# A streaming encoder step on one core: where the sample's projection stands in TensorE's order within an ada block

## The chip, the cores and the metric

One Trainium2 chip, one core of it. The metric is device time in microseconds (us), lower is better; every time below is of that core. TensorE is PE in the profile, its weight loads PEld, VectorE DVE, ScalarE ACT, GpSimd POOL, SyncE SP (which issues the DMAs).

## What is computed

One layer of a hybrid encoder, for a prompt of 512 tokens and a sample of 64 tokens, width 2048, all in float32:

```python
shift, scale, gate = split(silu(c) @ W_ada + b_ada)          # one row for the prompt, one for the sample
h = rmsnorm(x) * (1 + scale) + shift
q, k, v, z_att, u_ssm, z_ssm, u_pool, z_pool = split(h @ W_in)
y = concat(rmsnorm(attention(q, k, v)) * silu(z_att),
           rmsnorm(s5(u_ssm)) * silu(z_ssm),
           rmsnorm(pool_mix(u_pool)) * silu(z_pool))
x = x + gate * (y @ W_out);  out = rmsnorm(x)
```

The change lies in the first stage, where shift, scale, h and the first six 128-wide tiles of `h @ W_in` are made.

## The kernel before, in words

Tokens lie along the free dimension, features on partitions: x is 16 blocks of 128 features by 576 tokens (512 prompt, 64 sample). A product with a large weight is made of three passes with the short float type: weight high times h high, weight low times h high, weight high times h low.

The first stage runs over the 16 feature blocks b (the loop at L447). Block b of h needs shift and scale of its own 128 features, and those need a product over all 2048 inputs: the **ada products** of block b, `ada_mm` (L324). They are 16 float32 matmuls, each with 32 columns of weights (silu(c), two columns of it in use) and 256 moving columns of W_ada; the sixteen are put on four column groups of the array (`pa[32 * g:...]`, L330), and each stands as two instructions in the trace, 32 in all. `ada_sel` (L333) copies the result out of PSUM (ScalarE, L336), transposes it in two matmuls (L338), adds the four groups with a VectorE reduce (L340) and makes scale and shift (L342, L343 through the helper at L73). `modulate` (L409) then makes block b of h: VectorE scales x (L419, helper L76) and makes `hs`, the sample's 64 columns (L421); ScalarE rounds to `hh` (L423); VectorE makes the rest `hl` (L425, helper L76).

`first_tiles(b, fs)` (L429) adds block b to the seven running sums. For f from 0 to 5 that is three matmuls with 128 weight columns and 512 moving columns (L436 to L438; tiles `fA`, `fB`, each of two halves, then `fC`, `fD`). For f = 6 it is the **sample's projection**: `hs` are the weights, in four groups of 32 columns, and 384 columns of W_in move (L442; four float32 matmuls, eight instructions, tile `fS`).

The order within a block is written out by hand: the loop stands under a manual schedule (L320) that keeps PE, SP, DVE and ACT in program order. `F1CUT` (L34) says which tiles stand in which of three places:

```python
        first_tiles(b, F1CUT[0])
        if b + 1 < KT:
            ada_mm(b + 1, 0)
            ada_mm(b + 1, 1)
        first_tiles(b, F1CUT[1])
        if b + 1 < KT:
            ada_sel(b + 1)
            modulate(b + 1)
        ...
        first_tiles(b, F1CUT[2])
```

So in block b stand, one after the other on PE, the tiles of `F1CUT[0]`, the ada products of block b + 1, the tiles of `F1CUT[1]`, the two transposes, the tiles of `F1CUT[2]`. Blocks 0 to 14 have ada products in them; block 15 has none.

Data: SP issues the ada tiles two blocks ahead (`load_ada`, L181, issued at L189: two of 1 MB for each block) and the block's 384 KB of W_in (`load_w1`, L174, issued at L178). An ada buffer is free again when the ada products that read it are done. ScalarE and VectorE split W_in into high and low ahead of the block (`split_w`, L379: `w1h` at L382, `w1l` through L70), and VectorE works off some of the scalar preparations of the S5 branch (`disc`, L247) at the end of each block. After the stage come attention, the S5 and pooling branches and the output projection, each with its own loops of three-pass matmuls (L500, L1118 to L1120).

Of the kernel before, what the change touches and what calls it, by code (L numbers as in the profile page):

```python
# [14 lines left out]
PSUM = bass.MemoryType.PSUM  # L15
# [17 lines left out]
PRE = 2  # L33
F1CUT = ((6, 0), (1,), (2, 3, 4, 5))  # L34
MANUAL = 0
# [13 lines left out]
def kernel(ctx, tc, xp, xs, xT, cT, wada_ss, wada_g, bsh, bsc, bgate, ng, wf1, wrest,  # L49
# [27 lines left out]

    # ---------------------------------------------------------------- constants
    ident = const.tile([128, 128], F32, name="ident")
# [20 lines left out]
    def rms_inv(pool, ssq, n, bias, hbias, shape, tag):  # L100
        """1/sqrt(ssq/n + bias), with a Newton step; hbias is -bias/2, bias may be None"""
        v = pool.tile(shape, F32, tag=tag + "v", name="v")
        s = pool.tile(shape, F32, tag=tag + "s", name="s")
        ts(v, ssq, -0.5 / n, hbias, ALU.mult, ALU.add)
        if bias is None:
            A.activation(s, v, AF.Sqrt, scale=-2.0)
        else:
            A.activation(s, ssq, AF.Sqrt, scale=1.0 / n, bias=bias)
        r = pool.tile(shape, F32, tag=tag + "r", name="r")
        V.reciprocal(r, s)  # L110
        mul(s, r, r)
        mul(s, s, v)
        stt(r, s, 1.5, r, ALU.add, ALU.mult)
        return r

    # ---------------------------------------------------------------- PSUM
    psctx = ExitStack()
# [5 lines left out]

    # ---------------------------------------------------------------- weights: loaded ahead, split into high and low
    wsrc = [wrest[r, :, 8 * h:8 * h + 8] for r in range(38) for h in range(2)]
# [34 lines left out]

    # ---------------------------------------------------------------- startup: x, modulation, first tiles
    hh, hl = [], []
# [183 lines left out]
    for b in range(PRE):  # L346
        load_ada(b)
    # 1/rms of each token, on every partition
    acc = [wp.tile([128, NT], F32, tag="wh", name="acc") for _ in range(2)]
# [14 lines left out]
    V.tensor_scalar(prm[:, 1], prm[:, 1], 1.0, None, op0=ALU.add)  # L364
    # keeps the array's clock up until the sums below
    warm = pp.tile([128, 2, 512], F32, tag="pj", name="warm")
# [62 lines left out]
    def first_tiles(b, fs):  # L429
        w, wh, wl, hs = blk[b]  # L430
        c, i = divmod(b, 4)
        f0, l0 = b == 0, b == KT - 1
        for f in fs:
            if f < 6:
                wsl = slice(128 * f, 128 * f + 128)
                PE.matmul(f1p[f], wh[:, wsl], hh[c][:, i, 0:NP], start=f0, stop=False)  # L436
                PE.matmul(f1p[f], wl[:, wsl], hh[c][:, i, 0:NP], start=False, stop=False)
                PE.matmul(f1p[f], wh[:, wsl], hl[c][:, i, 0:NP], start=False, stop=l0)  # L438
            else:
                # the sample tokens token-major: a column group for each half of the tokens and of the features  # L440
                for g in range(4):
                    PE.matmul(fS[32 * g:32 * g + 32], hs[:, 32 * (g // 2):32 * (g // 2) + 32],  # L442
                              w[:, 384 * (g % 2):384 * (g % 2) + 384], start=f0, stop=l0, skip_group_check=True)
# [40 lines left out]

    # a projected tile: pieces (psum view, first token, count)
    def f1_pieces(f):
# [4 lines left out]
    def proj_steps(done):  # L491
        """one projected tile, a yield after each sixteenth; then done(psum)"""
        ps = pp.tile([128, 2, 512], F32, tag="pj", name="pj")
        for k in range(KT):
            if k % 8 == 0:
                wh, wl = w_next(8)
            c, i = divmod(k, 4)
            for ws, hs, first, last in ((wh, hh, True, False), (wh, hl, False, False), (wl, hh, False, True)):
                for ch in range(2):
                    PE.matmul(ps[:, ch, 0:HC], ws[:, k % 8], hs[c][:, i, HC * ch:HC * ch + HC],  # L500
                              start=(k == 0 and first), stop=(k == KT - 1 and last))
            if k == KT - 1:
                nxt = done(ps)
                if callable(nxt):
                    pend.append(nxt)
            yield
            if k in (2, 7, 12) and pend:
                nxt = pend.pop(0)()
                if callable(nxt):
                    pend.append(nxt)  # L510
# [4 lines left out]
    def interleave(gens, units, total):  # L515
        """runs the steps of gens with the units spread over the first `total` of them"""
        n, done = 0, 0
        for g in gens:
            for _ in g:
                n += 1  # L520
                while done < len(units) and done * total < n * len(units):
                    units[done]()
                    done += 1
        while done < len(units):
            units[done]()
            done += 1

    # ---------------------------------------------------------------- attention
    at = ExitStack()
# [192 lines left out]

    # ---------------------------------------------------------------- S5 branch, with the gates z beside it
    zs = ExitStack()
# [4 lines left out]
    def branch_rstd(tiles, ssq, width, out):  # L729
        """out[:, t] = 1/sqrt(sum over features / width + eps), on every partition"""  # L730
        v, s = tiles
        for ch in range(2):
            ps = mtile("bps", (128, HC))
            cs = slice(HC * ch, HC * ch + HC)
            PE.matmul(ps, ones, ssq[:, cs], start=True, stop=True)  # L735
            ts(v[:, cs], ps, 1.0 / width, EPS, ALU.mult, ALU.add)
        A.activation(s, v, AF.Ln)
        A.activation(out, s, AF.Exp, scale=-0.5)
        mul(s, out, out)
        stt(s, s, -0.5, v, ALU.mult, ALU.mult)  # L740
        stt(out, s, 1.5, out, ALU.add, ALU.mult)
# [14 lines left out]
    def s5_units(q):  # L756
# [3 lines left out]
        def op_x():  # L760
            ER = ck("ER", F32, (128, 2304))
            bc = ER[:, 1728:2240].rearrange("p (z a c) -> p z a c", z=4, a=4)
            for z, src in enumerate((sbr, sbi, scr, sci)):
# [4 lines left out]
                      E=[ER[:, 576 * z:576 * z + 576].rearrange("p (a j) -> p a j", a=4) for z in range(3)])  # L768
            # X[state, s, (g, c)] = a^(3-s) coef b
            X = s5.tile([128, 2, 4, 4, 32], F32, tag="X", name="X")  # L770
# [16 lines left out]
        def op_c():  # L787
            # C[state, tau, (g, c)] = c a^tau (imaginary part negated)
            tA, tB, bc = t_["tA"], t_["tB"], t_["bc"]
# [7 lines left out]
        def op_e(part):  # L797
            # E_j = e^(i phi (j+1)); the third row holds the decay, with resets
            E, tA, tB = t_["E"], t_["tA"], t_["tB"]
# [13 lines left out]
        def op_k():  # L813
            # taps of the chunk's own inputs: K[(f, g, c), tau, (g, c')], the skip added to tap 0
            X, Ct = t_["X"], t_["Ct"]
# [13 lines left out]
        def op_g(fp):  # L829
            # inputs of the chunks, rotated  # L830
            E, tA, tB, XT = t_["E"], t_["tA"], t_["tB"], t_["XT"]
# [73 lines left out]

    # pooling
    cinv = zp.tile([128, 16], F32, name="cinv")
# [135 lines left out]

    # ---------------------------------------------------------------- output projection and final norm
    pf = ctx.enter_context(tc.tile_pool(name="pf", bufs=8, space=PSUM, reuse_waits="tile"))
# [104 lines left out]
    def out_gate(t, po, n, cs=slice(0, 512)):  # L1150
        """x + gate * product"""
        out_mul(t, po, n, cs)
        out_add(t, n, cs)
# [5 lines left out]
    def out_sum(t):  # L1159
        """the mean of the first three sums of squares, with eps, and that times -1/2"""  # L1160
        m = 128 if t < 4 else 64
# [10 lines left out]
    def out_scale(t, r, c, act=False):  # L1172
        """columns 512 c on: times r, and in the last group times the gain"""
        xv = xo[t][0:128 if t < 4 else 64, 512 * c:512 * c + 512]
        if c == 3:
            stt(xv, xv, r[:, 0:1], gfs[3][0:128 if t < 4 else 64], ALU.mult, ALU.mult)
        elif act:
            A.activation(xv, xv, AF.Copy, scale=r[:, 0:1])
        else:
            V.tensor_scalar(xv, xv, r[:, 0:1], None, op0=ALU.mult)  # L1180
# [16 lines left out]

    # in the last group the tiles end one after the other, the last one in two halves
    po = {t: pf.tile([128, 512], F32, tag="f", name="po2") for t in range(5)}
# [5 lines left out]
    with tc.manual_schedule(engines={getattr(mybir.EngineType, e) for e in LASTENG}):  # L1205
        r = {}
# [49 lines left out]
def _layout(i):  # L1256
# [31 lines left out]

    # groups g = 2 (4 f + q) + g2 -> partition (g2, state), column (q, f)
    def gs(a):  # L1290
        r = a.reshape((4, 4, 2) + a.shape[1:])          # f q g2 s ...
        return np.moveaxis(r, [2, 3, 1, 0], [0, 1, 2, 3])  # g2 s q f ...

# [68 lines left out]
```

## Time and profile before

| what | value |
|---|---|
| median of 3 runs | 1043.99 us (1043.7 to 1044.51) |
| span of the profiled execution | 1042.7 us |
| the profiled execution's own time | not listed; the runs lie 1.0 to 1.8 us above the span |
| PE busy | 1011.0 us, 97% of the span |
| DVE, ACT, POOL busy | 710.5, 460.3, 4.2 us |
| mean granted clock of PE | 0.993 of full |
| ada stage | from about 29 to 148 us |

Read it from the top down: first which engine fills the span, then whether it does so in the stage of the change too, then the order of time of one block of that stage. An engine's busy time counts for the end only where the others wait for it. The ends of matmuls are modelled, so distances between starts are used for what a matmul takes.

### The profile page before, as it was taken

Reading aid. Unit: us, or ns where it says so; the run is one execution under the profiler, and the core shown is the slowest. Engines: PE = TensorE matmul, PEld = TensorE weight load, DVE = VectorE, ACT = ScalarE, POOL = GpSimd, SP = SyncE. Lnnn points to the kernel's source line nnn. Section 1 sums busy time; section 2 is a strip of 40 time slices with the busy share of each in tenths; the row PEclk is TensorE's granted clock in tenths of the full one; section 3 lists DMA queues with packets and bytes.
Section 4 is the critical chain, followed back from the end, with each engine's and each line's share of the span. In section 5 each row is a group of like instructions: output and inputs, shape, how many; then the busy total and the mean of one; then the engine's idle time right before and its main releaser. Section 6 shows DMA issues by size and latency. Waiting matters only on the chain. (4 is left out here: it accounts for less than half of the span.)

```text
span 1042.7 us, 17908 instructions
## 1 busy us (share of the span) xinstructions
PE 1011.0 (97%) x7048; PEld 904.0 (87%) x7048; DVE 710.5 (68%) x1678; ACT 460.3 (44%) x913; POOL 4.2 (0%) x36
## 2 busy tenths in 40 slices
PE   4999999999999999999999999999999999999996
PEld 3556579999999999999989999998999988888885
DVE  5476777656454655645589797886444669988786
ACT  5232355546344535444653644657453513222325
POOL 0000000000000000000000000000000000000000
PEclk8999999999999999999999999999999999999999
DMA  9998833233232233222212322221322596746525
GB/s 365 411 352 327 325 116 116 89 93 98 80 110 84 87 104 99 72 82 73 66 60 81 92 81 71 76 79 42 102 81 82 172 307 207 227 157 192 151 91 192
DMA packets 51572, 148.44 MB, mean 142 GB/s; under 512 B 9313, under 2 KB 18529, under 8 KB 46817
## 3 DMA queue, kind: packets, MB, share of 16 engines
q1 hardware_dynamic: 51488, 147.31, 42.8%
q8 instruction: 55, 0.90, 0.4%
q14 instruction: 29, 0.23, 0.1%
HBM read 137.75 MB, written 9.53 MB: 141 GB/s over the span
## 5 line engine op out<-in xcount | busy, mean ns | idle before, releaser
L500 PE MATMUL pj<-hh,wh 128*128 128x288 f32 x1344 | 299.0, 304 | 0.5 <-DVE Q L76 0.5
L500 PE MATMUL pj<-hh,wl 128*128 128x288 f32 x1344 | 287.8, 296 | 0.0
L500 PE MATMUL pj<-hl,wh 128*128 128x288 f32 x1344 | 287.3, 295 | 0.0
L500 PEld LDWEIGHTS pj<-hh,wh 128*128 128x128 f32 x1344 | 214.6, 189 | 5.5 <-issue 0.8
L500 PEld LDWEIGHTS pj<-hh,wl 128*128 128x128 f32 x1344 | 216.0, 188 | 0.1
L500 PEld LDWEIGHTS pj<-hl,wh 128*128 128x128 f32 x1344 | 215.7, 188 | 0.1
L146 ACT CAST wh<-w 128x1024 fp32r<-128x1024 f32 x120 | 125.8, 1050 | 198.3 <-PE po L1122 86.2
L70 DVE TENSOR_TENSOR wl<-w,wh 128x1024 fp32r<-128x1024 f32 x120 | 146.6, 1222 | 94.0 <-ACT wh L146 93.0
L1119 PE MATMUL po<-wl,yh 128*128 128x512 f32 (+1 forms) x256 | 99.1, 387 | 0.0
L1120 PE MATMUL po<-wh,yl 128*128 128x512 f32 (+1 forms) x256 | 99.0, 387 | 0.0
L1118 PE MATMUL po<-wh,yh 128*128 128x512 f32 (+1 forms) x256 | 98.7, 387 | 0.0
L76 DVE SCALAR_TENSOR_TENSOR acc<-ada,scT,acc 128x512 f32<-128x512 f32 x120 | 83.0, 744 | 0.5
L621 ACT ACTIVATE P<-P,s 128x128 f32<-128x128 f32 (+4 forms) x80 | 43.3, 541 | 77.2 <-DVE s L620 76.9
L618 DVE CUSTOM_DVE_ANT_0 P<-sps,Tb 128x128 f32<-128x128 f32 (+4 forms) x80 | 36.5, 458 | 36.7 <-PE sps L614 22.6
L1118 PEld LDWEIGHTS po<-wh,yh 128*128 128x128 f32 x256 | 48.1, 188 | 9.9
L1120 PEld LDWEIGHTS po<-wh,yl 128*128 128x128 f32 x256 | 48.1, 188 | 9.8
L1119 PEld LDWEIGHTS po<-wl,yh 128*128 128x128 f32 x256 | 48.1, 188 | 9.8
L622 DVE RECIPROCAL s<-s 128x1 f32<-128x1 f32 (+1 forms) x80 | 12.8, 161 | 43.1 <-ACT P L621 42.4
L623 DVE TENSOR_SCALAR P<-P,s 128x128 f32<-128x128 f32 (+4 forms) x80 | 29.5, 370 | 2.3
L423 ACT ACTIVATE hh<-xc,m 128x512 fp32r<-128x512 f32 (+1 forms) x32 | 15.4, 528 | 34.4 <-DVE xc L76 34.4
L67 DVE TENSOR_TENSOR ssqa<-ssqa,sq 128x576 f32<-128x576 f32 x7 | 5.3, 756 | 35.8 <-ACT sq L666 35.8
L70 DVE TENSOR_TENSOR K<-kv,K 64x704 fp32r<-64x704 f32 x32 | 28.2, 883 | 0.5
(338 smaller groups left out, 1427.0 us busy)
## 6 DMA issues: line engine op xcount, KB each, us to landing
w<-in_wrest_dram SPq DMA_DIRECT2D x84, 512.0 KB, 3.7
ada<-in_wada_ss_dram SPq DMA_DIRECT2D x22, 1024.0 KB, 7.1
w<-in_wout_dram SPq DMA_DIRECT2D x32, 512.0 KB, 4.2
ada<-in_wada_g_dram SPq DMA_DIRECT2D x32, 512.0 KB, 4.4
adac<-in_wada_ss_dram SPq DMA_DIRECT2D x10, 1024.0 KB, 11.2
w<-in_wf_dram SPq DMA_DIRECT2D x16, 384.0 KB, 8.1
xc<-in_xT_dram SPq DMA_DIRECT2D x8, 576.0 KB, 7.3
Tb<-in_ext_dram SPq DMA_DIRECT2D x8, 512.0 KB, 3.9
```

The source lines that it names most:

```text
L70: V.tensor_tensor(o, a, b, op=ALU.subtract)
L76: V.scalar_tensor_tensor(o, in0=a, scalar=s, in1=b, op0=op0, op1=op1)
L146: A.copy(wh, t)
L423: A.activation(hh[c][:, i, tk], xv[:, tk], AF.Identity, bias=m4[:, t:t + 1])
L500: PE.matmul(ps[:, ch, 0:HC], ws[:, k % 8], hs[c][:, i, HC * ch:HC * ch + HC], start=(k == 0 and first), stop=(k == KT - 1 and last))
L618: V.tensor_tensor_reduce(out=p[0:n, 0:nk], in0=ps[0:n], in1=Tb[0:n, h, ::-1][:, b0:b0 + nk], scale=1.0, scalar=-3.0e38, op0=ALU.add, op1=A ...
L621: A.activation(p[0:n, 0:nk], p[0:n, 0:nk], AF.Exp, bias=s4[0:n, 1:2], accum_out=s4[0:n, 2:3])
L622: V.reciprocal(s4[0:n, 3:4], s4[0:n, 2:3])
L623: V.tensor_scalar(p[0:n, 0:nk], p[0:n, 0:nk], s4[0:n, 3:4], None, op0=ALU.mult)
L1118: PE.matmul(po[t], yh[c][:, ci, s_], wh[:, i], start=f0, stop=False)
L1119: PE.matmul(po[t], yh[c][:, ci, s_], wl[:, i], start=False, stop=False)
L1120: PE.matmul(po[t], yl[c][:, ci, s_], wh[:, i], start=False, stop=l0)
```

## The change

The sample's projection stays first. Tile 0 goes from before the ada products to behind them, and tile 1 from before the two transposes to behind them. The rest of the diff takes out comments.

```diff
-F1CUT = ((6, 0), (1,), (2, 3, 4, 5))
+F1CUT = ((6,), (0,), (1, 2, 3, 4, 5))
```

PE's order in a block of index b, before and after:

```
before: sample(b), tile 0, ada(b+1), tile 1, transposes(b+1), tiles 2 3 4 5
after:  sample(b), ada(b+1), tile 0, transposes(b+1), tiles 1 2 3 4 5
```

## Rows read from the trace of the kernel before

**Rows 1.** The page, part 1: busy time, share of the span, instructions

```profile
PE 1011.0 (97%) x7048; PEld 904.0 (87%) x7048; DVE 710.5 (68%) x1678; ACT 460.3 (44%) x913; POOL 4.2 (0%) x36
```

**Rows 2.** Windows: stretch, length, busy (count) by engine, PEclk, DMA share, GB/s

```profile
22.10:25.60 3.50, 3.50 (x33) 1.38 (x32) 2.79 (x11) 0.93 (x2) 0.00 (x0) 0.50 1.02 422
...
27.30:30.70 3.40, 1.55 (x15) 0.62 (x13) 1.79 (x6) 1.27 (x3) 0.00 (x0) 0.99 1.02 422
30.70:34.10 3.40, 3.20 (x19) 1.59 (x23) 1.91 (x3) 1.11 (x3) 0.00 (x0) 0.51 1.04 378
...
61.21:68.61 7.40, 7.40 (x62) 4.50 (x61) 5.53 (x22) 2.06 (x5) 0.00 (x0) 1.00 1.01 422
...
34.20:1037.00 1002.80, 993.57 (x6937) 891.48 (x6929) 692.05 (x1638) 443.94 (x886) 3.02 (x29) 1.00 0.41 134
```

**Rows 3.** Timeline of PE in block 4: start, length, instructions, count

```profile
59.76 0.39 PE L436 MATMUL fC<-hh,w1h 128*128 128x512 f32 x1
...
60.44 0.39 PE L436 MATMUL fD<-hh,w1h 128*128 128x512 f32 x1
...
61.21 0.53 PE L442 MATMUL fS<-w,hs 128*32 128x384 f32 x4
...
61.55 0.51 PE L442 MATMUL fS<-w,hs 128*32 128x384 f32 x4
61.99 0.50 PE L436 MATMUL fA<-hh,w1h 128*128 128x512 f32 x1
...
62.88 0.42 PE L330 MATMUL pa<-adac,sc 128*32 128x256 f32 x4
...
64.42 0.40 PE L330 MATMUL pa<-adac,sc 128*32 128x256 f32 x4
64.75 0.50 PE L436 MATMUL fA<-hh,w1h 128*128 128x512 f32 x1
...
65.56 0.38 PE L338 MATMUL pa<-ident,S 128*128 128x128 f32 x2
```

**Rows 4.** Timeline of block 0, PE and PEld, to the start of block 1

```profile
29.49 0.85 PE L442 MATMUL fS<-w,hs 128*32 128x384 f32 x8 [1.49 <-DVE hs L421]
30.90 0.80 PE L436 MATMUL fA<-hh,w1h 128*128 128x512 f32 x1 [0.56 <-ACT hh L423]
...
32.48 2.73 PE L330 MATMUL pa<-ada,sc 128*32 128x256 f32 x32
...
32.91 0.20 PEld L330 LDWEIGHTS pa<-ada,sc 128*32 128x32 f32 x4 [0.23 <-issue]
33.34 0.20 PEld L330 LDWEIGHTS pa<-ada,sc 128*32 128x32 f32 x4 [0.23 <-issue]
...
35.94 0.38 PE L338 MATMUL pa<-ident,S 128*128 128x128 f32 x2
...
39.01 0.85 PE L442 MATMUL fS<-w,hs 128*32 128x384 f32 x8
```

**Rows 5.** Tiles ada and adac: issue and landing of the loads for blocks 1 and 2

```profile
L189 SPq DMA_DIRECT2D ada<-in_wada_ss_dram x2: 328/382/437, 15.6 to 15.9; - x2
...
DMA to landing us min/median/max: 8.5/9.6/10.7
...
L189 SPq DMA_DIRECT2D adac<-in_wada_ss_dram x2: 430/430/430, 16.9 to 17.4; - x2
...
DMA to landing us min/median/max: 13.2/14.8/16.5
```

**Rows 6.** Timeline of DVE in block 13, its fullest block of the stage

```profile
131.59 0.96 DVE L70 TENSOR_TENSOR w1l<-w,w1h 128x768 fp32r<-128x768 f32 x1
132.68 0.17 DVE L340 TENSOR_REDUCE m<-pa 128x4 f32<-128x16 f32 x1
...
134.33 0.25 DVE L421 TENSOR_SCALAR hs<-xc,m 128x64 f32<-128x64 f32 x1
```

**Rows 7.** PE's waits after the stage: the longest, in total, times, longest

```profile
PE km L819 <- DVE Ct L76: 2.4, 1, 2.4
```

## The prediction, made blind

> **What bounds the kernel now.** The page comes first: PE is busy for 97% of the span, and the next engine, VectorE, for 68% [rows 1]. The windows show whether that holds in the stage of the change: from 34.2 to 1037 us PE is busy 993.57 of 1002.80 us at a granted clock of 1.00, and one ada block takes 7.40 us with PE busy in all of it [rows 2]. The longest wait of PE behind the stage is 2.4 us on VectorE [rows 7], and none of its long waits there is for a DMA. So a microsecond less on PE in an ada block should be one less at the end. Where in a block PE's time goes is read from the starts of the timeline [rows 3]; block 0, before which PE still waits and the clock changes, has a timeline of its own [rows 4].
>
> **What a border costs.** A full tile (three passes of 512 columns) takes 0.68 us among its like: 59.76 to 60.44. The ada products come in groups of four column groups, all four started at once; from 62.88 to 64.42 lie seven groups, 0.22 us each for 256 moving columns. The sample's groups move 384 columns, so 0.22 x 384 / 256 = 0.33 us, and the first is followed after 0.34 us (61.21, 61.55). But from the second to tile 0 behind it 0.44 us pass, 0.11 us over its pace [rows 3]. Tile 0 between two narrow neighbours takes 62.88 - 61.99 = 0.89 us, 0.21 us more than 0.68. Going from 32-column work to 128-column work and back thus costs about 0.32 us, and a block does it twice: once for the sample, once for the ada products.
>
> **What the change does, part by part.** Nothing is added or removed. Tile 0 (three matmuls, three weight loads) moves behind the 32 ada instructions; tile 1 moves behind the two transposes. Neither issues a DMA or a wait of its own on SP or GpSimd; the other engines keep their order.
>
> Blocks 1 to 14. Before, from the second sample group to the first ada group: 62.88 - 61.55 = 1.33 us. After, this is one step between two narrow streams, and the tile taken out of it stands among full tiles at 0.68 us. The step is shown by no row. Its lower end is the pace of the sample's columns, 0.33 us; its upper end is the dearest border here, 0.44 us. I take 0.33, because within the ada products one 32-column group follows another at the pace of its columns, and that is the nearest row. The saving is 1.33 - 0.33 - 0.68 = 0.32 us a block (0.21 at the upper end), and 14 x 0.32 = 4.5 us. From the ada products to the transposes three full matmuls stand as before (64.75 to 65.56), so the copy of the products has the same cover as now, and that step costs nothing.
>
> Block 0. PE starts the sample at 29.49, waits 0.56 us for the rounded block 0, and starts ada at 32.48 [rows 4]. After, ada needs no block 0 and fills that wait: its data, issued by 15.9, landed at most 10.7 us later, by 26.6 [rows 5]. It starts near 29.49 + 0.34 + 0.33 = 30.16. At 30.7 the clock falls to about half (0.51 until 34.1 [rows 2]); I leave that fall where it is. Then 2.5 groups run at 0.22 us and 5.5 at 0.43 (32.91 to 33.34, [rows 4]), until 33.1. Tile 0 in the half clock took 1.58 us with its border (30.90 to 32.48); a little of it falls past 34.1, so the transposes start near 34.45. From there to the next block's sample it is 39.01 - 35.94 + 0.68 = 3.75 us: 38.2 in place of 39.01, a gain of 0.8 us.
>
> Waits that could open. *The ada data* is wanted earlier, by up to 0.9 us within a block and by the sum gained so far. The tightest is block 2's: issued by 17.4, landed at most 16.5 us later, so by 33.9 [rows 5], and wanted at 38.2 + 0.67 = 38.9. Later tiles are issued when an ada buffer is freed, which the change brings forward too. A block's 2.5 MB (two loads of 1 MB and 384 KB) in 7.08 us would be 350 GB/s where 422 were moved [rows 2]. *VectorE* works in order. In block 13 the split of the weights ended at 132.55, 0.13 us before the reduce that waits behind it [rows 6]. Counted from the start of the block's sample, the transposes come about 1 us earlier after the change, while the split comes only about 0.7 us earlier, since it hangs on the modulate of the block before; so the reduce comes some 0.2 us later than the transposes allow. Behind it stands the chain to `hs`, 1.9 us (132.68 to 134.58), then the next sample. Cover: 3.75 us between transposes and sample, against 0.5 + 0.2 + 1.9 = 2.6 us. Cost nothing; without that cover it would be at most 0.2 us in such a block. The reads of `hh` and `hl` by tile 0 come later than now, behind ada.
>
> Sum: 4.5 + 0.8 = 5.3 us. The profiled span becomes 1042.7 - 5.3 = 1037.4. The median lies 1.3 us above that span; kept, this gives **1038.7 us**.
>
> **Rivals.**
>
> *The border stays dear (0.15).* The step from the sample's groups to ada costs 0.44 us, like the border to full-width work. Then 14 x 0.21 + 0.7 = 3.6 us: 1040.4. For it: no row shows two different narrow streams side by side. Against: inside ada every group changes its weights and its moving tile at no cost. The Trainium skill, "TensorE: Matmul & The Clock Gate", section "Part 3: Packing small matmuls — row/col tiling", says that a weight load overlaps a running matmul only if their row groups differ; all of these use all 128 rows, so by that rule the loads of the new border would be exposed and the time would be this rival's. By that rule the loads within ada would be exposed too, and the trace does not agree: 0.22 us per group leaves no room for them. The same skill's "TensorEngine Tiling (Array Packing)", section "Key Properties", has it that a change of the tiling mode, not of the tile, drains the array; by that the new border would cost nothing, and no run here shows it.
>
> *The clock does not fall at 30.7 (0.11).* It fell after 3.40 us in which PE was busy for 1.55 [rows 2]; now ada adds half a microsecond of work to that. Kept at full, ada ends near 32.0, tile 0 at 32.8 (0.81, 64.75 to 65.56 [rows 3]), block 1 starts at 32.8 + 3.75 = 36.55: block 0 gains 2.5 instead of 0.8, in all 7.0 us: 1037.0. That it stays low for another such stretch instead (0.04) would lose 3.4 / 2 = 1.7 us: 1040.4.
>
> *Slower: the narrow work in one piece lets the clock fall in the middle of the stage (0.03).* Sample and ada make one piece of 2.55 us in each block, where the longest was 1.87 us. For it: in 22.1 to 25.6 PE did nothing but ada work, and the clock stayed at 0.50, half of full, that is 1.2 for 2.4 GHz [rows 2]. A low stretch like the one at 30.7 costs 3.4 / 2 = 1.7 us, so the sign turns at 4 of them in the 14 blocks; one in each would cost 24 us: 1062. Against: the same two pieces stood 0.89 us apart in every block, and the clock stayed at 1.00 throughout.
>
> *No gain that shows (0.05).* The time comes back downstream, as longer waits of PE such as the one of 2.4 us on VectorE [rows 7]. VectorE's work there starts from PE's own results, so it moves along; for the whole gain to be lost, work tied to neither would have to set the end. That gives about 1043.
>
> **How the numbers follow.** Forecast 0.62, the rivals as given. What a measurement of this kernel can tell from no change is about 0.2%, 2.1 us, so faster begins below 1041.9: forecast, dear border and both clock cases of block 0 are on that side, 0.92. Within 0.2%: 0.05. Slower: 0.03. The range goes from the case without the fall (1037.0) to the dear border (1040.4), with 0.1 to 0.2 us of spread at either end: 1036.9 to 1040.6. The likeliest case alone would be 1038.0 to 1039.4.
>
> **What the profile after would show.** Block period 7.08 us instead of 7.40, with PE busy throughout; first ada group 0.33 us after the second sample group (0.44: the dear border); tile 1 at 0.68 us; in block 0 ada from about 30.2; block 1's sample near 38.2; everything behind the stage the same, 5.3 us earlier. I would be wrong if PE showed idle time in front of ada or the sample, if PEclk were below 1 in the stage after 35 us, or if PE's waits after the stage grew by as much as the stage shrank.

## The result and the profile after

The changed kernel took **1035.42 us** in the median of its first four runs (1035.32 to 1038.11), the kernel before beside it 1043.85 (1041.89 to 1044.51): ratio 0.993, 95% interval 0.9916 to 0.9944. By the medians that is 8.4 us less where 5.3 were forecast, and 1.5 us under the range's lower end. The ratio is taken over all the runs and is not the quotient of the medians (0.9919); by the means of these runs the two kernels lie 7.5 us apart. A second measurement gave 1036.64 against 1043.83, ratio 0.9937 (0.9923 to 0.995).

Executions of one and the same program differ by the stretches in which PE is granted half its clock. Over 105 runs beside the experiments the kernel before lay between 1040.5 and 1048.1 us, and by the mean granted clock that each run lists it orders itself: 1040.9 on average at 0.998 (8 runs), 1042.4 at 0.996 (22), 1043.8 at 0.994 (23), 1045.4 at 0.992 (15). The ten runs of the changed kernel do the same: 1035.5 at 0.996 (5 runs), 1037.8 at 0.994 (2), 1038.1 at 0.992 (1). At the same granted clock the two are 6.0 to 7.3 us apart (with one to five runs of the changed kernel at each level).

The page after, against [rows 1]: the span is 9.6 us shorter, and PE is busy for 8.0 us less with the same 7048 matmul instructions.

```profile
span 1033.1 us, 17910 instructions
...
PE 1003.0 (97%) x7048; PEld 905.1 (88%) x7048; DVE 710.7 (69%) x1678; ACT 460.3 (45%) x913; POOL 4.2 (0%) x36
```

Windows of the changed kernel (columns as in [rows 2]): two stretches ahead of block 0, block 0, block 2 of the steady ones, and all the rest.

```profile
21.50:24.80 3.30, 3.30 (x33) 1.44 (x25) 2.65 (x11) 0.94 (x3) 0.00 (x0) 0.50 1.02 425
24.90:28.20 3.30, 1.81 (x20) 1.38 (x24) 1.59 (x6) 0.96 (x3) 0.00 (x0) 1.00 1.03 422
27.80:34.86 7.06, 7.06 (x60) 4.68 (x61) 5.26 (x12) 3.17 (x7) 0.00 (x0) 1.00 1.03 399
48.99:56.06 7.07, 7.07 (x61) 4.67 (x61) 5.48 (x21) 2.06 (x4) 0.00 (x0) 1.00 1.01 416
34.86:1028.00 993.14, 983.74 (x6901) 890.51 (x6900) 690.14 (x1631) 443.09 (x883) 3.03 (x29) 1.00 0.41 135
```

A block takes 7.07 us with PE busy in all of it, where it took 7.40; after 24.9 us the clock stays at 1.00. (A mean of 1.00 over 993 us could hide a short fall; read in slices of a few us, the trace has none before 1028.) The timeline of PE, with one row of its weight loads, in block 2 of the changed kernel shows the new border (start, length, instructions, as in [rows 3]):

```profile
48.99 0.53 PE L442 MATMUL fS<-w,hs 128*32 128x384 f32 x4
49.34 0.51 PE L442 MATMUL fS<-w,hs 128*32 128x384 f32 x4
49.34 0.13 PEld L330 LDWEIGHTS pa<-ada,sc 128*32 128x32 f32 x4 [0.19 <-issue]
49.66 0.40 PE L330 MATMUL pa<-ada,sc 128*32 128x256 f32 x4
...
51.50 0.50 PE L436 MATMUL fA<-hh,w1h 128*128 128x512 f32 x1
...
52.30 0.38 PE L338 MATMUL pa<-ident,S 128*128 128x128 f32 x2
52.44 0.47 PE L436 MATMUL fA<-hh,w1h 128*128 128x512 f32 x1
```

From the second sample group to the first ada group it is 0.32 us, the pace of 384 columns: the border is free. The first ada weights are loaded at 49.34, while the sample's second group runs. At the two borders of tile 0 in block 4 of the kernel before, the weights were loaded only as the matmul itself began:

```profile
61.99 0.19 PEld L436 LDWEIGHTS fA<-hh,w1h 128*128 128x128 f32 x1 [0.62 <-ACT w1h L382]
...
62.88 0.12 PEld L330 LDWEIGHTS pa<-adac,sc 128*32 128x32 f32 x3 [0.36 <-issue]
```

Whether the late load is what such a border costs, or only goes with it, no run separates. A wait for ScalarE's `w1h`, which the first row names, it is not: in block 15 of the kernel before the last `w1h` ended 7.6 us ahead of tile 0, and the step is 0.44 us there too. From tile 0 behind ada (51.50) to the transposes (52.30) nothing changed: 0.80 us, where it was 0.81. Block 0 of the changed kernel, against [rows 4]:

```profile
27.80 0.85 PE L442 MATMUL fS<-w,hs 128*32 128x384 f32 x8 [1.49 <-DVE hs L421]
28.47 1.91 PE L330 MATMUL pa<-ada,sc 128*32 128x256 f32 x32
30.31 0.50 PE L436 MATMUL fA<-hh,w1h 128*128 128x512 f32 x1
...
31.12 0.38 PE L338 MATMUL pa<-ident,S 128*128 128x128 f32 x2
...
34.86 0.53 PE L442 MATMUL fS<-w,hs 128*32 128x384 f32 x4
```

Ada fills the wait for the rounded block, and the clock does not fall: 7.06 us to the next sample where it was 9.52. The sample itself starts 1.69 us earlier than in [rows 4]. The instructions of PE up to there are the same in both kernels, and in the first experiment below the changed kernel itself starts the sample at 29.40: this is a difference between executions, not the change's. Lastly the start of attention, PE first in the kernel before, then in the changed one:

```profile
148.92 0.61 PE L593 MATMUL pv<-ident,kv 128*128 128x128 f32 x4
149.50 0.27 PE L595 MATMUL pw<-ident,kv 128*64 128x128 f32 x1
150.22 0.50 PE L500 MATMUL pj<-hh,wh 128*128 128x288 f32 x2 [0.45 <-DVE Q L76]
```

```profile
140.05 0.51 PE L500 MATMUL pj<-hh,wh 128*128 128x288 f32 x2
...
141.72 0.60 PE L593 MATMUL pv<-ident,kv 128*128 128x128 f32 x4
142.15 0.27 PE L595 MATMUL pw<-ident,kv 128*64 128x128 f32 x1
142.18 0.51 PE L500 MATMUL pj<-hh,wh 128*128 128x288 f32 x2
```

The order of PE is written by hand in the first stage; at the start of attention a scheduler sets it, and for the changed program two steps of the projection came out ahead of the value transposes. The 0.45 us wait is gone. From the end of the stage (the first matmul of `fT`) to the first taps' product (`km`) it is 382.92 us instead of 383.55.

The span's 9.6 us are thus, but for rounding: 1.69 start, 2.46 block 0, 4.69 from block 1's sample to block 15's, 0.63 start of attention, and 0.2 in the wait for `ssqp` (2.0 instead of 2.2 us).

### The profile page after: what moved, and what is told of

Read it like the earlier page. It is cut to its first block, busy times and chain, and to the rows that moved or that the text cites. A ratio compares the mean times of both kernels' runs of the same rounds, so it can differ in the third digit from the quotient of the medians.

```text
span 1033.1 us, 17910 instructions
## 1 busy us (share of the span) xinstructions
PE 1003.0 (97%) x7048; PEld 905.1 (88%) x7048; DVE 710.7 (69%) x1678; ACT 460.3 (45%) x913; POOL 4.2 (0%) x36
```

## The experiments

Theory A: the order is worth 6.4 to 6.6 us at the same clock (1.3 block 0, 4.7 blocks 1 to 14, 0.6 attention), and the rest of the 8.4 is the clock, which falls in some executions and not in others. Its first version had 0.9 for block 0 and 6.3 in all; the 1.3 was read from the third experiment. Theory B: all 8.4 belong to the change. Times are medians of each kernel's own runs; ratios are to the kernel before in the same session. Experiments 1 to 4, 5 to 8, 9 to 11, 12, and 13 with 14 are five sessions, each on another chip.

**1. The changed kernel again**, unchanged.

> The changed kernel once more, beside the kernel before. Theory A: the change itself is worth about 6.3 us (4.7 in blocks 1 to 14, 0.9 in block 0, 0.6 to 0.8 at the start of attention, where the order of PE differs too); the other 2 us of the first measurement are the clock of PE in the first 35 us, which differs between executions of one and the same program. Then both kernels show two levels about 2.2 to 2.7 us apart (before near 1041.9 and 1044.1, after near 1035.4 and 1038.1), and like is 6.0 to 6.6 us from like. Theory B: the change itself takes away the falls of the clock at the start; then the kernel before stays near 1044 and this one near 1035.4 in nearly all runs.

Measured: 1036.64 (1035.35 to 1038.11), 7.2 us below the kernel before beside it. Theory A's two levels didn't show, and the kernel before did not stay near 1044 as theory B has it: it spread over 1040.8 to 1046.3. The windows of this execution's profile, two ahead of block 0, block 0, and all the rest:

```profile
20.30:27.00 6.70, 6.70 (x48) 4.50 (x47) 2.79 (x11) 1.30 (x3) 0.00 (x0) 0.50 1.03 423
27.10:30.40 3.30, 1.81 (x24) 1.10 (x27) 1.79 (x6) 1.06 (x3) 0.00 (x0) 1.00 1.02 420
29.40:36.45 7.05, 7.05 (x60) 4.67 (x61) 5.34 (x13) 3.74 (x7) 0.00 (x0) 1.00 1.03 398
30.50:1030.00 999.50, 989.93 (x6948) 894.65 (x6940) 694.85 (x1642) 445.68 (x889) 3.03 (x29) 1.00 0.41 136
```

This is the same program as above, but the first low stretch lasted to 27.0, as in the kernel before, and the sample of block 0 came at 29.40. There the clock fell at 30.7 in [rows 2]; here it stayed at 1.00. So in this start too block 0 took 7.05 us. The 1.69 us of the start are between executions. The fall at 30.7 did not come in a start like that one once ada filled PE's wait. The fifth and sixth experiment have a second such pair, the third a start in the old order without the fall.

**2. The new order in block 0 alone.**

```diff
...
+        F1CUT = F1NEW if b == 0 else F1OLD
...
```

`F1OLD` is the order of the kernel before, `F1NEW` that of the changed one.

> The new order in block 0 alone; blocks 1 to 14 keep the old one, and so does the start of attention. Both theories: block period 7.40 in blocks 1 to 14. Theory A: 0.8 to 1.0 us below the kernel before at the same clock of the start (1041.0 or 1043.2). Theory B: 2.5 us or more below it in nearly every run (1041.5 or less, even where the kernel before is at 1044).

Measured: 1043.68 against 1043.83, ratio 1.0005 (0.9993 to 1.0016). Theory B asked for 1041.5 or less, so block 0 doesn't hold the excess. Theory A's gain of about 1 us doesn't show in the medians, but ten of its twelve runs were at 0.992 or 0.993, and there they average 1043.99 (six runs, 0.992) and 1043.76 (four, 0.993) where the kernel before has 1045.39 and 1044.86 (15 and 17 runs). Where the clock went is in the windows: block 0, block 1, and two stretches of the S5 stage.

```profile
27.86:34.91 7.05, 7.05 (x60) 4.67 (x60) 5.26 (x12) 3.02 (x6) 0.00 (x0) 1.00 1.03 397
34.91:42.31 7.40, 7.40 (x61) 4.49 (x60) 3.10 (x8) 2.31 (x5) 0.00 (x0) 1.00 1.02 418
531.20:534.50 3.30, 3.30 (x15) 3.30 (x15) 3.30 (x9) 0.00 (x0) 0.00 (x0) 0.50 0.25 58
705.30:708.50 3.20, 3.20 (x15) 3.20 (x15) 3.20 (x6) 0.43 (x3) 0.00 (x0) 0.50 0.24 58
```

The clock fell behind each of the two long waits of PE, for `Ct` (VectorE's operand of the taps' product, 2.4 us) and for `ssqp` (the pooling branch's sum of squares, 2.1 us). The kernel before has both (2.4 us in [rows 7], and 2.2), but with no fall in its profile. From the first taps' product to the last matmul that reads weights low and `ysp` (L1123 of the kernel before) it took 488.5 us here, 485.5 there.

**3. The new order in blocks 1 to 14 alone.**

```diff
...
+        F1CUT = F1NEW if b >= 1 else F1OLD
...
```

> The old order in block 0, the new one in blocks 1 to 14; the start of attention as in the changed kernel. Theory A: 4.7 us from the blocks (period 7.07) and 0.6 to 0.8 from the start of attention, 5.4 us below the kernel before at the same clock of the start: 1036.5 or 1038.7. Theory B: the falls of the clock stay, so nearly always 1038.7, 3.3 us above the changed kernel.

Measured: 1039.51, ratio 0.9962 (0.995 to 0.9974), 4.3 us below the kernel before; 5.0 to 5.9 below it at 0.993 and 0.992, as theory A has it. Its windows show block 0 in the old order at full clock, a block in the new one, and the wait for `Ct` with the stretch behind it:

```profile
27.85:36.21 8.36, 7.74 (x61) 4.49 (x61) 4.66 (x11) 3.16 (x7) 0.00 (x0) 1.00 1.02 401
36.21:43.28 7.07, 7.07 (x62) 4.68 (x61) 4.40 (x12) 2.65 (x5) 0.00 (x0) 1.00 1.02 418
524.00:527.20 3.20, 1.33 (x15) 1.13 (x16) 3.20 (x7) 0.24 (x1) 0.00 (x0) 1.00 0.13 54
527.30:530.60 3.30, 3.30 (x15) 3.30 (x15) 3.30 (x9) 0.00 (x0) 0.00 (x0) 0.50 0.30 60
```

Block 0 in the old order takes 8.36 us at full clock: the new order saves 1.3 there, and the fall at 30.7 cost 9.52 - 8.36 = 1.16 on top. The start of attention had the changed kernel's order here and took its 382.91 us; the second experiment had the old order and its 383.55. So the 0.6 us hang on that order.

By the medians alone the two parts don't add up: 0.15 us for block 0 and 4.3 for the rest, where the whole change has 7.2 in the same session. The runs of these two kernels had the lower clock, 0.992 on average, against 0.994 for the kernel before and 0.995 for the changed one. At equal clock the parts are 1.1 to 1.4 and 5.0 to 5.9.

**4. The neighbourhood without the cover.** Tile 0 first, then sample and ada.

```diff
-F1CUT = ((6, 0), (1,), (2, 3, 4, 5))
+F1CUT = ((0, 6), (1,), (2, 3, 4, 5))
```

> Tile 0, then sample and ada next to each other, tile 1, transposes: the neighbourhood without tile 0 behind ada. If the neighbourhood alone makes the saving in the blocks: period 7.07 as in the changed kernel, and in block 0 PE still waits for the rounded block. If it is tile 0's place that counts (more cover behind ada): period 7.2 to 7.4.

Measured: 1043.77 against 1043.83, ratio 1.0002 (0.9993 to 1.0011): no gain in the medians. The period was 7.25 us, so that 14 blocks still gained 2.2 us; the runs, all at 0.989 to 0.993, don't show it, but at 0.992 and 0.993 (three runs each) they average 1043.4 and 1043.2 against 1045.4 and 1044.9. The timeline of a block's start and PEld's waits over 40 to 140 us say why the period is not 7.07:

```profile
68.45 0.39 PE L436 MATMUL fA<-hh,w1h 128*128 128x512 f32 x1
...
68.68 0.39 PE L437 MATMUL fA<-hh,w1l 128*128 128x512 f32 x1
69.00 0.19 PEld L438 LDWEIGHTS fA<-hl,w1h 128*128 128x128 f32 x1 [0.35 <-DVE hl L76]
69.00 0.50 PE L438 MATMUL fA<-hl,w1h 128*128 128x512 f32 x1
69.43 0.52 PE L442 MATMUL fS<-w,hs 128*32 128x384 f32 x3
```

```profile
PEld fA L438 <- DVE hl L76: 4.9, 14, 0.4
```

With tile 0 at the head, its third matmul needs `hl` 0.45 us into the block and waits for VectorE in every block: it starts 0.32 us behind the second, where the second came 0.23 behind the first, and the sample 0.43 behind it, where in the kernel before 0.33 lay between a full tile's third matmul and narrow work (62.56 to 62.88). That is 0.2 us, the difference between the periods. In block 0 PE waited for the rounded block before anything else, and the clock was at 0.50 from 28.9 to 35.5. So the narrow pieces next to each other keep about half of the saving; for all of it they must stand first as well, where they cover the chain to `hh` and `hl`.

**5 and 6. The two long waits of the S5 stage taken away by order**, in either kernel: the taps' product one unit later, the pooling scale one hop later.

```diff
-        return [op_x, op_c, op_xt, lambda: op_e(0), op_k, lambda: op_e(1), lambda: op_e(2), lambda: op_g(0),
+        return [op_x, op_c, op_xt, lambda: op_e(0), lambda: op_e(1), op_k, lambda: op_e(2), lambda: op_g(0),
...
-        return pool_scale if g == 3 else None
+        return (lambda: pool_scale) if g == 3 else None
```

> The kernel before, with its two long waits of PE in the S5 stage taken away by order alone: the taps' product one unit later, the pooling scale one hop later. If the scatter of the runs comes from falls of PE's clock at these waits (they are there in the profiles of the second and third experiment, not in those of the kernel before and after): 2.4 + 2.0 us less, so about 1039.3, and fewer levels among its runs; only the start still scatters. If the waits only move elsewhere: 1041 to 1044 and the scatter as before.

> The changed kernel with the same two waits taken away. Theory A (the change is worth 6.4 at the same clock: 1.3 block 0, 4.7 blocks 1 to 14, 0.6 start of attention): 6.4 to 7.6 us below the kernel before with the same edit, the upper end if ada in block 0 also spares the second fall of the clock at the start (1.2 us where it happens). About 1031 to 1032.5. Theory B (all of 8.4 is the change's): 8.4 below it.

Measured: 1048.58, ratio 1.0055 (1.0037 to 1.0074), and 1039.74, ratio 0.9975 (0.9961 to 0.999); 8.8 apart, above theory A's bound of 7.6 and nearer to theory B (7.9 by the means). None of the forecast times came: the fifth was 5.8 us slower than the kernel before beside it, the sixth 3.1 and 4.3 slower than the changed kernel's two medians. PE's waits in the fifth show that they only moved, one to `H`, one to the pooling product:

```profile
PE po L954 <- issue: 5.0, 1, 5.0
PE yp L877 <- ACT H L865: 2.2, 1, 2.2
```

The fall in block 0 stands in the fifth's profile again, and not in the sixth's. First the fifth, old order: block 0 and the stretch of the fall; then the sixth, new order: block 0.

```profile
28.65:38.18 9.53, 8.97 (x60) 5.02 (x61) 4.69 (x11) 3.19 (x7) 0.00 (x0) 0.82 1.02 403
29.90:33.30 3.40, 3.23 (x19) 1.59 (x23) 1.91 (x3) 1.07 (x3) 0.00 (x0) 0.50 1.05 389
```

```profile
28.05:35.11 7.06, 7.06 (x61) 4.67 (x61) 5.25 (x12) 3.28 (x7) 0.00 (x0) 1.00 1.03 399
```

**7 and 8. The same pair with matmuls that nobody reads in PE's idle time at the start.**

```diff
-WARM = 12
+WARM = 18
...
+    PE.matmul(fA[:, 0, 0:384], ident, xc[3][:, WLANE, 0:384], start=True, stop=True)
```

> As the fifth experiment, with extra matmuls at the start whose results nobody reads: six more of the ones that keep the clock up ahead of the sums, and one of 384 columns into the gap ahead of block 0. If PE's idle time at the start is what lets the clock fall: mean granted clock nearer 1 than in the fifth, no fall after block 0, 1 to 3 us less than it. If the falls come all the same: the same time or up to 1 us more.

> As the sixth experiment, with the same extra matmuls. With the clock's part out of both, this kernel and the seventh should differ by what the order alone does: 1.3 + 4.7 + 0.6 = 6.6 us, within 0.5. If the difference stays at 8 or more, the order does more than the profiles show. It should be the fastest of all: 1029 to 1032.

Measured: 1047.18, ratio 1.0036 (1.0017 to 1.0054), and 1041.11, ratio 0.998 (0.9966 to 0.9995); 6.1 apart, inside what theory A gave. In both profiles the clock stood at 1.00 from about 18 us on, through the stage; block 0 took 8.37 and 7.06, the blocks 7.402 and 7.064 us, the way from the stage's end to the first taps' product 387.56 and 386.94. The sum of these differences is 6.66. That the eighth would be the fastest of all, 1029 to 1032, was wrong; it carries the waits of the fifth and sixth. And the same extra matmuls that went with 1.4 us less in the seventh than in the fifth went with 1.4 us more in the eighth than in the sixth.

**9 and 10. The S5 stage's order as it was, its waits filled instead**, besides the start: two matmuls of 384 columns ahead of the second half of the taps' product, four of 224 ahead of the pooling sums.

```diff
+                    for _ in range(2):
+                        PE.matmul(kmb[:, 128:512], ident, X[:, 0, 0:3].rearrange("p a s c -> p (a s c)"), start=True, stop=True, skip_group_check=True)
...
+                for _ in range(4):
+                    PE.matmul(psb[:, HC:512], ident, ypool[0][:, 0, 0:512 - HC], start=True, stop=True, skip_group_check=True)
```

> The order of before, with matmuls that nobody reads in PE's idle time: at the start as in the seventh experiment, and in the two long waits of the S5 stage (two of 384 columns, four of 224), whose order stays. If falls of the clock make the scatter: all runs within 1 us, at the kernel before's lowest level less what the start gains, 1038.5 to 1041. If the scatter has another source: 1041 to 1046 as before.

> The new order with the same fillers. The profiles of the seventh and eighth kernel give for the order alone: 1.3 (block 0 at full clock) + 14 x 0.335 = 4.7 + 0.6 (start of attention) = 6.6 us; so 6.1 to 7.0 below the ninth, 1032 to 1034.5, with little scatter. If the order is worth the 8.4 of the first measurement even with the clock held: 1030 to 1032.

Measured: 1049.47, ratio 1.0056 (1.0039 to 1.0073), and 1042.96, ratio 0.9994 (0.9978 to 1.0009). The difference, 6.5, is theory A's, but both levels are far above the forecast: the second filler read `y_pool`, which VectorE writes late, so the wait before it grew to 4.6 us and the clock fell behind it. Nor did the fillers always hold the clock of the start: in the tenth's profile it was at 0.50 from 23.3 to 26.7.

**11 and 12. The fillers of the start alone**, with the new order and with the old one.

> The new order with the fillers of the start alone. The change itself has already filled block 0; what is left is the fall ahead of it. So 0.4 to 2 us below the changed kernel: 1033.3 to 1035.5; the clock still falls in some runs at the two waits of the S5 stage (3 us for both), which the tenth should not show.

> The order of before with the fillers of the start alone, partner of the eleventh kernel (1035.28). With the clock of the start held in both, the order alone is left: 6.4 to 6.7 us, so 1041.7 to 1042.0 in the middle, up to 1.7 more per fall of the clock at the waits of the S5 stage; block 0 near 8.37, its neighbours 7.40. If the order alone were worth 8.4: 1043.7 with the clock of the start at full in the profile.

Measured: 1035.28 (1034.95 to 1036.9), ratio 0.9924 (0.9909 to 0.9939), and 1043.91 (1042.84 to 1046.32), ratio 0.9997 (0.9983 to 1.0011). They are 8.6 apart, which speaks for theory B; but they come from two sessions on two chips, and the six runs of the eleventh were at 0.995 to 0.998, the twelve of the twelfth at 0.993 to 0.996. The eleventh came out inside its forecast of 1033.3 to 1035.5, but that is no gain that shows on the changed kernel's 1035.42. In the twelfth's profile the clock fell behind both waits of the S5 stage, in the eleventh's behind one.

**13 and 14. All of it held, and no instruction moved**: as 9 and 10, the second filler of the identity.

```diff
-                for _ in range(4):
-                    PE.matmul(psb[:, HC:512], ident, ypool[0][:, 0, 0:512 - HC], start=True, stop=True, skip_group_check=True)
+                for _ in range(9):
+                    PE.matmul(psb[:, 384:512], ident, ident, start=True, stop=True, skip_group_check=True)
```

> The order of before with fillers at the start and in both waits of the S5 stage, this time of data that is there (the identity), so that no instruction changes its place. If the falls of the clock at these waits make the scatter: no fall at 531 and 705 in the profile, runs within 1.5 us, about 1041 (the lowest level of the kernel before, 1040.5 to 1041, with less fall at the start).

> The new order with the same fillers. If the order alone is worth 6.6 us (1.3 + 4.7 + 0.6) and what went beyond it in the first measurement was the clock: 6.1 to 7.1 below the thirteenth kernel, about 1034.4. If the new order itself spares falls at the S5 waits, or does more than the profiles show: more than 7.5 below it with the clock held in both.

Measured: 1045.06 (1041.23 to 1047.72), ratio 1.0007 (0.9994 to 1.0019), and 1035.86 (1034.64 to 1039.66), ratio 0.9937 (0.9921 to 0.9953): 9.2 apart in the medians (7.5 in the means), outside theory A's bound, and the thirteenth's runs spread over 6.5 us where 1.5 were forecast. But in most runs of the thirteenth the clock was not held: three of its twelve were at 0.998, and three of the fourteenth's six. Those average 1041.95 and 1035.34, 6.6 apart. The profiles of both are of such runs; here the thirteenth's windows, then the fourteenth's: block 0, block 1, from the stage's end to the taps, the rest.

```profile
27.00:35.37 8.37, 7.75 (x61) 4.49 (x62) 4.68 (x11) 3.31 (x7) 0.00 (x0) 1.00 1.03 406
35.37:42.77 7.40, 7.40 (x62) 4.49 (x62) 3.67 (x10) 2.14 (x5) 0.00 (x0) 1.00 1.02 420
143.98:527.51 383.53, 383.08 (x2901) 364.05 (x2899) 221.34 (x614) 196.92 (x431) 2.35 (x24) 1.00 0.30 90
527.51:1035.00 507.49, 500.84 (x3157) 460.21 (x3156) 394.45 (x757) 213.93 (x391) 0.33 (x3) 1.00 0.40 127
```

```profile
26.91:33.97 7.06, 7.06 (x61) 4.67 (x61) 5.25 (x12) 3.13 (x6) 0.00 (x0) 1.00 1.03 403
33.97:41.04 7.07, 7.07 (x61) 4.67 (x61) 3.70 (x9) 2.40 (x5) 0.00 (x0) 1.00 1.01 415
137.91:520.84 382.93, 382.78 (x2901) 364.06 (x2899) 221.28 (x613) 196.51 (x430) 2.30 (x24) 1.00 0.30 90
520.84:1028.00 507.16, 500.59 (x3157) 460.11 (x3156) 394.49 (x757) 213.93 (x391) 0.33 (x3) 1.00 0.40 127
```

With the clock at 1.00 in every row, in slices of a few us too: 1.31 in block 0, 14 x 0.334 = 4.68 in the blocks, 0.60 at the start of attention, 6.6 in all. The spans, 1039.8 and 1032.4, differ by 0.8 more: waits of 0.35 us for `ssqp` and a few tenths at the output's weights that one execution has and the other has not.

**What stays open.** The order alone is worth 6.6 us: the profiles of 7 and 8, of 9 and 10 and of 13 and 14 give 6.6 to 6.7 for block 0, the blocks and the start of attention together, those of 11 and 12 give 6.5, and the comparison at equal granted clock agrees. The medians of the seven pairs differ by 6.1, 6.5, 7.2, 8.4, 8.6, 8.8 and 9.2, their means by 5.9 to 8.4. What a single pair of executions has beyond 6.6 can be set against the time for which PE stood at half clock before the output's end; half of that time is taken as lost, an estimate as in the prediction:

| profiles, old and new order | spans apart (us) | at half clock, old and new (us) | spans apart, less half the difference |
|---|---|---|---|
| before, changed | 9.6 | 10.2, 3.4 | 6.2 |
| 5, 6 | 10.0 | 13.7, 6.8 | 6.6 |
| 7, 8 | 6.4 | 10.2, 10.2 | 6.4 |
| 9, 10 | 2.6 | 3.4, 10.2 | 6.0 |
| 12, 11 | 7.7 | 6.8, 3.4 | 6.0 |
| 13, 14 | 7.5 | 0, 0 | 7.5 |

Whether the new order itself makes the clock fall less often is not settled. For it: in the old order, with nothing added at the start, the clock fell in block 0 in the profiles of the kernel before and of the fifth experiment; with the new order there it fell in none of four (changed kernel, first, second, sixth). Against: in the third experiment's profile block 0 had the old order too, and no fall came. Of the falls at the S5 waits these runs don't show that either order meets fewer by more than chance. Why the clock fell in most runs of the thirteenth kernel no trace shows, since its profile is of a run without a fall.

## Why the prediction was wrong

- **The border and the blocks: right.** 0.33 us forecast, 0.32 measured; period 7.08 forecast, 7.07 measured; 4.5 us forecast, 4.7 measured. By the rule on row groups that stood beside the rival of a dear border (the Trainium skill, "TensorE: Matmul & The Clock Gate", "Part 3: Packing small matmuls — row/col tiling") the loads at the border could not have run under the sample's matmuls; the trace doesn't agree with it (49.34, above). With the rule that only a change of the tiling mode drains the array ("TensorEngine Tiling (Array Packing)", "Key Properties", the Trainium skill again) the trace agrees: 0.32 us at the border within the mode, as fast as the columns go; 0.33 us from the last ada group to full-width work (51.17 to 51.50), where a group's pace is 0.22.
- **No new wait: right.** PE is busy for all of 7.06 and 7.07 us in blocks 0 and 2; neither ada data nor `hs` is waited for behind block 0. The fourth experiment shows what the cover is worth.
- **Block 0: the step that failed first.** "I leave that fall where it is": in the profile of the changed kernel the clock did not fall, and block 0 gained 2.46 us instead of 0.8. The rival of 0.11 came true in its own size (2.5). Of it 1.3 is the order at full clock and 1.16 the fall.
- **"Everything behind the stage the same": wrong by 0.6 us.** The sum put nothing there. The order at the start of attention is not written by hand, and a change ahead of it moved it.
- **The median from one span: wrong twice, in opposite ways.** The sum was made against a span of 1042.7 with 1.3 us around it. Every run lists 2.3 us more than its span (1035.37 for 1033.1), so the profiled execution of before took about 1045.0, above all three runs shown: it was one with much low clock, from 20.5 to 27.3 ahead of block 0, where the changed kernel's had it from 21.5 to 24.9. That is the 1.69 us of the start. The range counted bounds of the change and none of this, while the kernel before alone spreads over 7 us.
- **How much of the result is chance.** At equal granted clock the order's 6.6 us would put the median near 1037.4, inside the range. That both medians of the changed kernel lie below the range goes with the clock that its ten runs were granted, 0.995 on average against 0.994; how much of that the change brought and how much was the draw of few runs stays open.
- **Slower by narrow work in one piece: refuted.** The clock stayed at 1.00 over 34.86 to 1028, with one piece of sample and ada in each block. And in 21.5 to 24.8 PE did little but ada work at 0.50, and the clock was at 1.00 from 24.9 on; the prediction had taken a row of the kernel before with the same work as a sign for this rival.

## What to carry to other kernels

Put work of one array mode together: going from 32-column to 128-column work and back cost about 0.32 us here, going from one 32-column stream to another nothing. Put it where the wide work still waits for its operands, or part of the gain is lost to that wait, as when tile 0 went first. Before a forecast of half a per cent, ask how far executions of the same program lie apart and why: here it is the granted clock, and the two kernels could be told apart to a microsecond only at the same one.

## What was not expected of the hardware

Long waits of PE can cost more than their length. Behind the wait of 2.4 us for `Ct` the clock was at 0.50 for over 3 us in the second, third and twelfth experiment's profiles, and not behind the same wait in those of the kernel before, the changed one and the first and eleventh experiment. Two such falls stretched the part behind the taps from 485.5 to 488.5 us.

That work which nobody reads gains time is not shown. With the start filled, the eleventh kernel's six runs had the lowest median of the study, 1035.28, and a spread of 2 us, but it is not clear of the changed kernel's own 1035.42 and 1036.64; the twelfth's 1043.91 is not clear of the kernel before beside it either (1044.17).
